# Branch products of a hybrid encoder layer: parts of 768 and 320 tokens, an ungated first state-space half, three PSUM banks beside the scan

## The chip, the cores and the metric

The kernel runs on one core of a Trainium2 chip. The metric is device microseconds for one execution of the whole layer. The kernel before has a median of 2577.64 us over 3 runs (2576.39 to 2583.05); the profiled execution, from which all rows below come, took 2582.58 us with a span of 2580.8 us from its first to its last instruction.

## The reference

One step of a one-layer encoder is computed for 1024 prompt tokens and 64 tokens of a running stream, T = 1088 tokens in all, with a model width of 1024. Cut to what matters here:

```
xn   = rmsnorm(x)
z | xBC | dt | q | k | v | g_ssm | g_att = xn @ w_in
xs, B, C = silu(causal_conv4(xBC))
y_ssm = rmsnorm_by_group( (SSD_scan(xs, dt, B, C) + d * xs) * silu(z) )       # 32 heads in 4 groups, 2048 wide
o     = rmsnorm( softmax(q1 k1) v - lam * softmax(q2 k2) v )                  # 8 heads, 1024 wide
mix   = sigmoid(g_ssm) * (y_ssm @ w_branch_ssm) + sigmoid(g_att) * (o @ w_branch_attn)
x     = x + mix @ w_out
x     = x + ConvFFN(rmsnorm(x))
```

The two branch products and the line `mix` are what the change touches. The kernel keeps tanh(g/2) of each gate, so that sigmoid(g) is (1 + tanh)/2; the factor 1/2 is applied after the output projection.

## The kernel before, in words

Data is kept transposed, with features on the 128 partitions and tokens along the free axis. Every large product is done in three matmuls of a split format: an operand a is rounded to a_hi, a_lo = a - a_hi, and `product` (L140) accumulates hi*hi, hi*lo and lo*hi in one PSUM bank. A weight block (128 x 1024) is loaded by `weights` (L125), cast on ScalarE (L136) and subtracted on VectorE (L137), two blocks deep.

The stages are: input norm, projections of values, queries and keys; attention (L478 on) with the remaining projections as filler; the state-space scan (L640 on) with the rest of the projections and then the branch products as filler; the third branch product; output projection and norm (L789 on); the feed-forward part (L825 on). The emission order gives priorities, and a scheduler decides at compile time in which order each engine's queue holds its instructions. On the chip each queue runs in that order; an instruction that waits holds up all behind it on its engine. All DMAs that matter here go through one queue, SyncE's (SP).

PSUM has eight banks. Two of them (`pm`, tag "mm") serve the large products everywhere; a third group of banks, `more`, is added in the first stage only. The helper `acc` (L112) hands out banks in turn. In the scan the pool `pss` holds six banks of one tile each: `tr` (transposed inputs), `cb` (transposed B, and C times B), `yi` and `ye` (outputs from within the chunk and from the state), `stp` (state update), and `gst` (the sums of squares for the norm by group).

The scan runs over 4 groups and, in each, over three spans of 384, 384 and 320 tokens: 12 spans, numbered 0 to 11. A span has three calls of `step` (L658; 128 tokens each, the last of a group 64) and one of `gated` (L714). A step transposes its inputs into `tr` and `cb`, copies `cb` out on ScalarE (L676), forms the decay matrix on GpSimd and ScalarE (L682, L684), multiplies it on VectorE (L685), and then does `yi`, `ye` and `stp`; VectorE gathers y (L697, L698) and the state (L709). `gated` adds d * xs on VectorE (L718), multiplies by the gate on GpSimd (L719), squares on ScalarE (L720), adds on GpSimd (L721, L722), sums over partitions on TensorE into `gst` (L724), takes the reciprocal root with ScalarE and VectorE (`rstd_of`, L212 to L217; the readers of `gst` are L212 and L214), scales y (L728) and stores it to y_sc. `fill` takes pieces of the filler between steps.

`branch` (L156) does one branch product: the 1088 tokens are cut into halves of 544, each output block m into two slices of 272 columns. It is called three times: for the attention (gated by g, stored to m_sc), for the first half of the state-space input (y_sc rows of groups 0 and 1; gated, m_sc added, stored to n_sc), both as filler in the scan, and for the second half after the scan (gated, n_sc added, split into `mix`). Its gate tiles and the tiles to be added come by DMA into `b_g`; `bring` loads and splits the input of a part. The evacuation of a slice is L196, the addition L198.

## Time and profile before

| | |
|---|---|
| median of 3 runs | 2577.64 us |
| profiled execution | 2582.58 us, span 2580.8 us |
| mean granted TensorE clock | 0.995 |
| VectorE busy | 1399.8 us (54%) |
| ScalarE busy | 1032.2 us (40%) |
| GpSimd busy | 290.0 us (11%) |
| HBM | 263.56 MB read, 100.27 MB written |

A row of the grouped view gives line, engine, operation, output and inputs, shapes and count, then busy time and mean of one in ns, then the engine's idle time just before these instructions and what ended it. A row of the view by windows gives, for a stretch in us from the start of the span, the busy time of each engine with its count of instructions, the granted clock and the share and rate of the DMA engines. Matmuls are pipelined: the duration of one contains the time in which the next is already running, so a rate is read from a count over a stretch. PE is the matrix engine, PEld its weight load, DVE is VectorE, ACT ScalarE, POOL GpSimd.

### The profile page before, as it was taken

The numbers are of one execution on the slowest core, as the hardware profiler recorded it, in microseconds if no ns is written. First come the engines' busy times: TensorE is split into PE (matmuls) and PEld (weight loads), VectorE is DVE, ScalarE is ACT, GpSimd is POOL, SyncE is SP. The second block draws the span as 40 slices with busy tenths as digits, with TensorE's granted clock in tenths as the row PEclk, the third lists the DMA queues.
The fourth block names the chain that finished last, engine by engine and source line by source line (L and its number), as shares of the span: only waits on it lengthen the run. The fifth ranks groups of instructions, "written<-read, shape, count | busy, mean of one in ns | idle before, by whom it ended". The sixth has DMA issues, their size and how long they took to land.

```text
span 2580.8 us, 41810 instructions
## 1 busy us (share of the span) xinstructions
PE 2525.0 (98%) x16484; PEld 2444.8 (95%) x16484; DVE 1399.8 (54%) x2371; ACT 1032.2 (40%) x2113; POOL 290.0 (11%) x387
## 2 busy tenths in 40 slices
PE   8999999999999999999999989999999999999999
PEld 7999999999999999988788879999999999999999
DVE  7326266654447674665679997658333333343333
ACT  5334234544445554565456643335312222131221
POOL 3000001000001110022333430023000000000000
PEclk9999999999999999999999999999999999999999
DMA  5217167545435433176798978555311111111112
GB/s 162 83 54 282 51 257 213 153 142 148 131 126 164 136 112 111 64 232 192 245 332 258 304 246 272 195 187 193 119 42 47 44 42 50 42 50 40 44 43 77
DMA packets 233685, 366.59 MB, mean 142 GB/s; under 512 B 31184, under 2 KB 160464, under 8 KB 233360
## 3 DMA queue, kind: packets, MB, share of 16 engines
q1 hardware_dynamic: 233488, 363.91, 44.2%
q8 instruction: 130, 2.13, 0.3%
q14 instruction: 67, 0.55, 0.1%
HBM read 263.56 MB, written 100.27 MB: 141 GB/s over the span
## 4 chain that ended last, share of the span: by engine, by line
PE 43%; DMA 3%; DVE 3%; ACT 1%; issue 1%; SPq 0%; POOL 0%; DVEq 0%; ACTq 0%; POOLq 0%
PE mm L143 7%; PE mm L145 7%; PE mm L144 7%; PE up L143 7%; PE up L145 7%; PE up L144 7%; DMA in<-x_sc 1%; DMA b_hi<-o_sc 1%; DVE w_lo L137 1%; PE yi L689 1%; PE stp L702 0%; ACT bc L684 0%; DVE y L728 0%; DMA in<-z_sc 0%; DVE b_lo L170 0%
## 5 line engine op out<-in xcount | busy, mean ns | idle before, releaser
L143 PE MATMUL mm<-xn_hi,w_hi 128*128 128x320 f32 (+1 forms) x1496 | 497.9, 333 | 2.3 <-ACT zr L428 1.1
L145 PE MATMUL mm<-xn_hi,w_lo 128*128 128x320 f32 (+1 forms) x1496 | 496.8, 332 | 0.0
L144 PE MATMUL mm<-xn_lo,w_hi 128*128 128x320 f32 (+1 forms) x1496 | 494.6, 331 | 0.0
L136 ACT CAST w_hi<-w_f 128x1024 fp32r<-128x1024 f32 (+2 forms) x220 | 229.3, 1042 | 547.2 <-PE mm L144 369.3
L137 DVE TENSOR_TENSOR w_lo<-w_f,w_hi 128x1024 fp32r<-128x1024 f32 (+2 forms) x220 | 284.9, 1295 | 300.8 <-ACT w_hi L136 298.4
L143 PE MATMUL up<-x_hi,w_hi 128*128 128x384 f32 (+1 forms) x1056 | 345.0, 327 | 2.7 <-ACT x_hi L820 2.7
L144 PE MATMUL up<-x_lo,w_hi 128*128 128x384 f32 (+1 forms) x1056 | 344.8, 327 | 0.0
L145 PE MATMUL up<-x_hi,w_lo 128*128 128x384 f32 (+1 forms) x1056 | 343.3, 327 | 0.0
L143 PEld LDWEIGHTS mm<-xn_hi,w_hi 128*128 128x128 f32 x1496 | 281.9, 188 | 7.9 <-issue 2.8
L145 PEld LDWEIGHTS mm<-xn_hi,w_lo 128*128 128x128 f32 x1496 | 281.6, 188 | 2.9 <-issue 1.9
L144 PEld LDWEIGHTS mm<-xn_lo,w_hi 128*128 128x128 f32 x1496 | 281.8, 188 | 2.6 <-issue 1.3
L143 PE MATMUL mm<-b_hi,w_hi 128*128 128x272 f32 x768 | 228.0, 298 | 19.1 <-DVE b_g L196 15.9
L144 PE MATMUL mm<-b_lo,w_hi 128*128 128x272 f32 x768 | 227.2, 296 | 0.7 <-DMA b_lo<-o_sc 0.7
L145 PE MATMUL mm<-b_hi,w_lo 128*128 128x272 f32 x768 | 227.5, 297 | 0.0
L143 PEld LDWEIGHTS up<-x_hi,w_hi 128*128 128x128 f32 x1056 | 198.7, 188 | 3.1 <-ACT x_hi L820 3.0
L144 PEld LDWEIGHTS up<-x_lo,w_hi 128*128 128x128 f32 x1056 | 198.8, 188 | 0.1
L145 PEld LDWEIGHTS up<-x_hi,w_lo 128*128 128x128 f32 x1056 | 198.5, 188 | 0.0
L880 DVE TENSOR_TENSOR xa<-xa,mm 128x384 f32<-128x384 f32 x144 | 76.5, 531 | 197.3 <-PE mm L145 197.3
L144 PE MATMUL mm<-f_lo,w_hi 128*128 128x384 f32 (+1 forms) x528 | 173.1, 328 | 0.0
L143 PE MATMUL mm<-f_hi,w_hi 128*128 128x384 f32 (+1 forms) x528 | 173.0, 328 | 0.0
L145 PE MATMUL mm<-f_hi,w_lo 128*128 128x384 f32 (+1 forms) x528 | 173.0, 328 | 0.0
L143 PEld LDWEIGHTS mm<-b_hi,w_hi 128*128 128x128 f32 x768 | 147.3, 192 | 25.4 <-DVE b_g L196 15.4
(252 smaller groups left out, 4803.7 us busy)
## 6 DMA issues: line engine op xcount, KB each, us to landing
w_f<-in_win_dram SPq DMA_DIRECT2D x76, 512.0 KB, 4.0
w_f<-in_wup_dram SPq DMA_DIRECT2D x44, 512.0 KB, 3.7
bc<-a_sc SPq DMA_DIRECT2D x32, 512.0 KB, 6.3
w_f<-in_wbs_dram SPq DMA_DIRECT2D x32, 512.0 KB, 4.2
b_g<-g_sc SPq DMA_DIRECT2D x48, 272.0 KB, 4.5
w_f<-in_wout_dram SPq DMA_DIRECT2D x24, 512.0 KB, 3.8
x_sc<-cc SPq DMA_DIRECT2D x48, 192.0 KB, 1.9
kh_t<-k_st SPq DMA_DIRECT2D x32, 272.0 KB, 6.9
```

Of the source, the lines that this page charges most:

```text
L136: S.copy(hi, w)
L137: V.tensor_tensor(out=lo, in0=w, in1=hi, op=ALU.subtract)
L143: PE.matmul(ps, a_hi, b_hi, start=i == 0, stop=False)
L144: PE.matmul(ps, a_hi, b_lo, start=False, stop=False)
L145: PE.matmul(ps, a_lo, b_hi, start=False, stop=i == n - 1)
L689: PE.matmul(yi[u : u + 64, e // 2, :L], xdt[:L, e], bc[:L, e, :L], start=True, stop=True)
L880: V.tensor_tensor(out=xa[:, m, c : c + w], in0=xa[:, m, c : c + w], in1=ps, op=ALU.add)
```

## The change

The branch products are cut into a part of 768 and one of 320 tokens, with slices of 384, 384 and 320 columns. The tiles b_hi and b_lo have one buffer for each part, where two buffers of 544 served both parts in turn. Each tensor that is read beside a product has a tile of its own (768 wide, six buffers, before 1088 wide and four). The second call stores its product without gate and addition, copied out of PSUM by ScalarE. The third call adds n_sc to its product, multiplies by the gate and adds m_sc: three operations on VectorE for each slice. A generator yields after each slice (384 or 320 columns), before after each block (544 columns); still 2.5 pieces are taken per scan step. In the scan `gst` no longer has a bank of its own but takes turns with `cb` in one bank, and the bank set free serves the large products as a third. From the third branch product on, all eight banks serve the large products in turn; before, two served products and five the up-projection.

```diff
+TWO = ((0, 768), (768, 320))
-BG = 4
+BG = 6
-UPB = 5
+BRANCH_STEPS = 2.5
...
-    more, at_bank = None, 0
+    more, at_bank = (None, 0), 0
...
     def acc(w):
         nonlocal at_bank
-        at_bank = (at_bank + 1) % 5
-        pool, tag = (more, "mx") if more is not None and at_bank < 3 else (pm, "mm")
+        pool, n = more
+        at_bank = (at_bank + 1) % (n + 2)
+        pool, tag = (pool, "mx") if at_bank < n else (pm, "mm")
...
+    def branch(stage, side, src, wts, gates, adds, out):
+
+        def octet(x):
+            w = TWO[x][1]
+            return [br.tile([P, 8, w], R32, name=f"{n}{x}", tag=f"{n}{x}") for n in ("b_hi", "b_lo")]
...
+            for a in range(0, w, 384):
+                n = min(384, w - a)
+                t = stage()[:, :n]
+                load(out=t, in_=src[P * k : P * (k + 1), c + a : c + a + n])
+                S.copy(hi[:, k, a : a + n], t)
+                V.tensor_tensor(out=lo[:, k, a : a + n], in0=t, in1=hi[:, k, a : a + n], op=ALU.subtract)
...
-                two = pair()
-                gt, at = two[:, :HALF], two[:, HALF:T]
-                first = load(out=gt, in_=g_sc[g0 + P * m : g0 + P * (m + 1), c : c + HALF])
-                if add is not None:
-                    load(out=at, in_=add[r, c : c + HALF])
+                beside = []
+                for d, r0 in ([(g_sc, gates)] if gates is not None else []) + [(d, 0) for d in adds]:
+                    t = side()[:, :w]
+                    first = load(out=t, in_=d[r0 + P * m : r0 + P * (m + 1), c : c + w])
+                    beside.append(t)
+                to = beside[0] if beside else side()[:, :w]
...
-                for a in (0, HALF // 2):
-                    q = slice(a, a + HALF // 2)
-                    ps = acc(HALF // 2)
+                for a in range(0, w, 384):
+                    q = slice(a, min(a + 384, w))
+                    ps = acc(q.stop - a)
                     product(ps, [(w_hi[:, k], w_lo[:, k], hi[:, k, q], lo[:, k, q]) for k in range(KT)])
                     with tc.high_priority(ahead):
-                        V.scalar_tensor_tensor(gt[:, q], gt[:, q], 1.0, ps, ALU.add, ALU.mult)
-                if add is not None:
-                    V.tensor_tensor(out=gt, in0=gt, in1=at, op=ALU.add)
-                out(m, c, gt)
-                yield
+                        if not beside:
+                            S.copy(to[:, q], ps)
+                        elif not adds:
+                            V.scalar_tensor_tensor(to[:, q], to[:, q], 1.0, ps, ALU.add, ALU.mult)
+                        else:
+                            V.tensor_tensor(out=beside[1][:, q], in0=beside[1][:, q], in1=ps, op=ALU.add)
+                    if adds:
+                        V.scalar_tensor_tensor(to[:, q], to[:, q], 1.0, beside[1][:, q], ALU.add, ALU.mult)
+                        V.tensor_tensor(out=to[:, q], in0=to[:, q], in1=beside[2][:, q], op=ALU.add)
+                    out(m, c + a, to[:, q])
+                    yield
...
     with tc.tile_pool(name="sp", bufs=1) as sp, tc.tile_pool(name="pss", bufs=1, space=PSUM) as pss:
+        more = pss, 1
...
-            ps = pss.tile([P, 512], F32, name="gst", tag="gst")[:, :w]
+            ps = pss.tile([P, 512], F32, name="gst", tag="cb")[:, :w]
...
-            yield from branch(None, pair, o_sc, wba, D, None, store(m_sc))
-            yield from branch(stage, pair, y_sc[:D], wbs[0], 0, m_sc, store(n_sc))
+            yield from branch(None, side, o_sc, wba, D, (), store(m_sc))
+            yield from branch(stage, side, y_sc[:D], wbs[0], None, (), store(n_sc))
...
-            fill(SCAN_STEPS)
+            fill(SCAN_STEPS if late is not None else BRANCH_STEPS)
         load(out=conv, in_=conv_o)
         run(filler)
+    more = None, 0
...
-    run(branch(stage, pair, y_sc[D:], wbs[1], 0, n_sc, mixed))
+    psf = ctx.enter_context(tc.tile_pool(name="psf", bufs=6, space=PSUM))
+    more = psf, 6
+    run(branch(stage, side, y_sc[D:], wbs[1], 0, (n_sc, m_sc), mixed))
...
-            ps = psf.tile([P, 512], F32, name="st2", tag="st2")[:, :w]
+            ps = acc(w)
...
-                ps = psf.tile([P, 512], F32, name="up", tag="up", bufs=UPB)[:, :w]
+                ps = acc(w)
```

More of the change, by code (lines that the diff above doesn't have):

```diff
@@ L154, in project, with bring @@
             yield
-    def branch(stage, pair, src, wts, g0, add, out):
-        def octet():
-            return [br.tile([P, 8, HALF], R32, name=n, tag=n, bufs=2) for n in ("b_hi", "b_lo")]
-        def bring(c, k, hi, lo):
+    def branch(stage, side, src, wts, gates, adds, out):
+        def octet(x):
+            w = TWO[x][1]
+            return [br.tile([P, 8, w], R32, name=f"{n}{x}", tag=f"{n}{x}") for n in ("b_hi", "b_lo")]
+        def bring(x, k, hi, lo):
+            c, w = TWO[x]
             if stage is None:
@@ L162, in bring @@
                 for u, t in enumerate((hi, lo)):
-                    load(out=t[:, k].bitcast(F32), in_=src[D * u + P * k : D * u + P * (k + 1), c : c + HALF])
+                    load(out=t[:, k].bitcast(F32), in_=src[D * u + P * k : D * u + P * (k + 1), c : c + w])
                 return
-            for a in (0, HALF // 2):
-                q = slice(a, a + HALF // 2)
-                t = stage()
-                load(out=t, in_=src[P * k : P * (k + 1), c + a : c + a + HALF // 2])
-                S.copy(hi[:, k, q], t)
-                V.tensor_tensor(out=lo[:, k, q], in0=t, in1=hi[:, k, q], op=ALU.subtract)
@@ L172, in branch @@
-        parts = [octet(), None]
+            for a in range(0, w, 384):
[4 more added lines that the diff above has]
+                V.tensor_tensor(out=lo[:, k, a : a + n], in0=t, in1=hi[:, k, a : a + n], op=ALU.subtract)
+        parts = [octet(0), None]
         for k in range(8):
             bring(0, k, *parts[0])
-        for x, c in enumerate((0, HALF)):
+        for x, (c, w) in enumerate(TWO):
@@ L176, in branch @@
             hi, lo = parts[x]
             if x == 0:
-                parts[1] = octet()
+                parts[1] = octet(1)
             for m in range(KT):
-                r = slice(P * m, P * (m + 1))
-                two = pair()
-                gt, at = two[:, :HALF], two[:, HALF:T]
-                first = load(out=gt, in_=g_sc[g0 + P * m : g0 + P * (m + 1), c : c + HALF])
-                if add is not None:
-                    load(out=at, in_=add[r, c : c + HALF])
+                beside = []
@@ L186, in branch @@
+                for d, r0 in ([(g_sc, gates)] if gates is not None else []) + [(d, 0) for d in adds]:
[3 more added lines that the diff above has]
+                to = beside[0] if beside else side()[:, :w]
                 w_hi, w_lo = weights(wts[m], KT, P)
                 if x == 0 and m >= LAG:
-                    with tc.issue_after(first.ins):
+                    with tc.issue_after(first.ins) if beside else ExitStack():
@@ L189, in branch @@
                         for k in range(8 * (m - LAG) // (8 - LAG), 8 * (m - LAG + 1) // (8 - LAG)):
-                            bring(HALF, k, *parts[1])
-                for a in (0, HALF // 2):
-                    q = slice(a, a + HALF // 2)
-                    ps = acc(HALF // 2)
+                            bring(1, k, *parts[1])
+                for a in range(0, w, 384):
+                    q = slice(a, min(a + 384, w))
+                    ps = acc(q.stop - a)
                     product(ps, [(w_hi[:, k], w_lo[:, k], hi[:, k, q], lo[:, k, q]) for k in range(KT)])
@@ L202, in store @@
+                    if adds:
[3 more added lines that the diff above has]
+                    yield
     def store(dst):
-        return lambda m, c, t: load(out=dst[P * m : P * (m + 1), c : c + HALF], in_=t)
+        return lambda m, c, t: load(out=dst[P * m : P * (m + 1), c : c + t.shape[1]], in_=t)
@@ L225, in hybrid_layer @@
     ps1 = s1.enter_context(tc.tile_pool(name="ps1", bufs=1, space=PSUM))
-    more = s1.enter_context(tc.tile_pool(name="psx", bufs=3, space=PSUM))
+    more = s1.enter_context(tc.tile_pool(name="psx", bufs=3, space=PSUM)), 3
     def stat(w):
@@ L408, in hybrid_layer @@
     s1.close()
-    more = None
+    more = None, 0
     ahead = AHEAD
@@ L750, in stage, with side @@
         def stage():
-            return bs.tile([P, HALF // 2], F32, name="b_f", tag="b_f", bufs=BF)
-        def pair():
-            return bs.tile([P, T], F32, name="b_g", tag="b_g", bufs=BG)
+            return bs.tile([P, 384], F32, name="b_f", tag="b_f", bufs=BF)
+        def side():
+            return bs.tile([P, 768], F32, name="b_g", tag="b_g", bufs=BG)
         def branch_tiles():
@@ L769, in hybrid_layer @@
                 filler, late = late, None
-            fill(SCAN_STEPS)
+            fill(SCAN_STEPS if late is not None else BRANCH_STEPS)
         load(out=conv, in_=conv_o)
         run(filler)
+    more = None, 0
     dq.release()
@@ L779, in mixed @@
     def mixed(m, c, t):
-        q = slice(c, c + HALF)
+        q = slice(c, c + t.shape[1])
         S.copy(mix[0][:, m, q], t)
         V.tensor_tensor(out=mix[1][:, m, q], in0=t, in1=mix[0][:, m, q], op=ALU.subtract)
-    run(branch(stage, pair, y_sc[D:], wbs[1], 0, n_sc, mixed))
+    psf = ctx.enter_context(tc.tile_pool(name="psf", bufs=6, space=PSUM))
+    more = psf, 6
+    run(branch(stage, side, y_sc[D:], wbs[1], 0, (n_sc, m_sc), mixed))
     bs.release()
@@ L791, in hybrid_layer @@
     x2_lo = x2_pool.tile([P, KT, T], R32, name="x2_lo")
-    psf = ctx.enter_context(tc.tile_pool(name="psf", bufs=1, space=PSUM))
     with tc.tile_pool(name="op", bufs=1) as op:
```

## The prediction

> **What bounds the kernel now.** I read the page first, then the view by windows, the waits, and last the rows of the scan one by one.

> ```profile
> span 2580.8 us, 41810 instructions
> PE 2525.0 (98%) x16484; PEld 2444.8 (95%) x16484; DVE 1399.8 (54%) x2371; ACT 1032.2 (40%) x2113; POOL 290.0 (11%) x387
> ```

> TensorE (PE) is busy for 98% of the span, and no other engine comes near. But busy isn't the same as fed at full rate, so the stretches are compared:

> ```profile
> core 0: us, PE busy (x) PEld busy (x) DVE busy (x) ACT busy (x) POOL busy (x), PEclk, DMA share, GB/s
> 1265.00:1420.00 155.00, 145.05 (x1133) 129.45 (x1134) 131.73 (x181) 90.18 (x185) 60.45 (x39) 0.97 0.94 301
> 1420.00:1595.00 175.00, 159.92 (x1246) 144.75 (x1244) 155.72 (x232) 86.86 (x171) 59.44 (x35) 0.98 0.84 274
> 1610.00:1690.00 80.00, 80.00 (x638) 80.00 (x637) 47.95 (x78) 25.40 (x35) 0.00 (x0) 1.00 0.56 184
> 1900.00:2500.00 600.00, 600.00 (x3636) 600.00 (x3635) 216.24 (x327) 138.11 (x213) 21.65 (x64) 1.00 0.15 45
> ```

> The third branch product (1610 to 1690) and the feed-forward part (1900 to 2500) leave PE no gap. The scan with branch products as filler (1265 to 1595) does: PE is busy 305 of 330 us, while VectorE is at 87% and the DMA engines at 0.84 to 0.94. So only the scan and the rate of the matmuls themselves can be improved, and only the scan can easily be made worse. The scan itself runs from its first transposition to its last sum of squares:

> ```profile
> L671 PE MATMUL tr<-con,in x144: 270/273/415, 1116.8 to 1529.4; 128*128 128x128 f32 x128, 128*64 128x128 f32 x16
> L724 PE MATMUL gst<-in,con x24: 430/484/845, 1167.5 to 1566.6; 128*128 128x384 f32 x16, 128*128 128x320 f32 x8
> ```

> From the sum of span 0 (1167.5) to that of span 11 (1566.6) there are 11 spans, so one takes 36.3 us. What PE waits for in it:

> ```profile
> PE mm L143 <- DVE b_g L196: 15.9, 8, 4.6
> PE tr L671 <- ACT in L653: 4.3, 5, 1.6
> PE cb L673 <- ACT b_cb L676: 2.5, 1, 2.5
> PE gst L724 <- POOL in L722: 1.5, 2, 0.9
> ```

> The largest wait is a branch product that finds both banks full because VectorE hasn't emptied one. The scan's own waits are small, since a step of the next span (tr, cb, the decay product) can be done while GpSimd and ScalarE still work on the norm of this one.

> **The change part by part.**

> *Fewer, wider matmuls.* There are 3 x 8 x 8 x 3 = 576 groups of one block, one slice of the contraction and one term. Each had four matmuls of 272 columns and now has 384, 384 and 320, the mix of the feed-forward part. By the windows, 80 us / 638 = 125.4 ns and 600 / 3636 = 165.0 ns. So 4 x 125.4 - 3 x 165.0 = 6.6 ns a group, 576 x 6.6 = 3.8 us saved. [...]

> *A third bank for filler, and ScalarE emptying the second product.* This takes at most the 15.9 us of the wait for L196. Branch 1 is still emptied by VectorE, so I take 14; bounds 0 and 16.

> *Work taken off VectorE.* The second product loses 32 evacuations and 16 additions:

> ```profile
> L196 DVE SCALAR_TENSOR_TENSOR b_g<-b_g,mm 128x272 f32<-128x272 f32 x96 | 41.0, 429 | 46.2 <-PE mm L145 45.5
> L198 DVE TENSOR_TENSOR b_g<-b_g 128x544 f32<-128x544 f32 x32 | 24.5, 764 | 0.7
> PE stp L702 <- DVE xw L681: 0.6, 1, 0.6
> PE yi L689 <- DVE bc L685: 1.6, 1, 1.6
> ```

> That is 32 x 0.429 + 16 x 0.764 = 26 us, and 32 loads of 272 KB fewer in the scan. But beside L196 VectorE ended PE's waits for some 2.5 us only (bc 1.6, xw 0.6, y 0.3), so I take 3 us; bounds 0 and 10. In the third product the additions come back as three operations a slice, 24 x 3 x about 0.55 us = 40 us, where 25 were before; VectorE is at 48 of 80 us there, so they are hidden. Without that cover they would cost the 15 us of difference.

> *The shared bank of `cb` and `gst`.* This is the edit that costs. A bank of one buffer is handed on in emission order, and `gated` of span i is emitted before the steps of span i+1. So the first `cb` of a span now waits until L212 and L214 have read the sum of the span before, and that sum comes only after the whole of `gated`. In the compiled order of the changed kernel every `gst` stands right ahead of the three `cb` of the next span; before, two or three of them stood ahead of it. Each span becomes one chain: cb, three steps, `gated`, gst, next cb. Its length, by the rows of before:

> ```profile
> L685 DVE TENSOR_TENSOR bc<-bc,b_cb 128x1024 f32<-128x1024 f32 x32 | 47.9, 1498 | 7.0 <-ACT b_cb L676 6.4 <-ACT bc L684 0.5
> L681 DVE TENSOR_TENSOR xdt<-tr,dt_tok 128x512 f32<-128x512 f32 x32 | 21.9, 683 | 28.8 <-PE tr L671 28.7
> L709 DVE TENSOR_TENSOR state<-state,stp 128x512 f32<-128x512 f32 x32 | 21.7, 678 | 10.2 <-PE stp L702 5.4 <-POOL state L707 4.9
> L697 DVE TENSOR_TENSOR y<-ye,e 128x512 f32<-128x512 f32 x28 | 19.1, 681 | 6.4 <-PE ye L696 4.9 <-DMA e<-e_sc 1.1 <-PE cb L673 0.4
> L698 DVE TENSOR_TENSOR y<-y,yi 128x512 f32<-128x512 f32 x28 | 19.0, 677 | 4.8 <-PE yi L689 4.8
> L718 DVE SCALAR_TENSOR_TENSOR y<-in,par,y 128x384 f32<-128x384 f32 x32 | 19.0, 653 | 0.1
> L728 DVE SCALAR_TENSOR_TENSOR y<-y,par,grs 128x384 f32<-128x384 f32 x32 | 20.4, 695 | 0.2
> L719 POOL TENSOR_TENSOR y<-y,in 128x1536 f32<-128x1536 f32 x8 | 29.6, 3706 | 11.7 <-DVE y L718 11.7
> L720 ACT ACTIVATE in<-y 128x1536 f32<-128x1536 f32 x8 | 11.9, 1484 | 12.1 <-POOL y L719 12.1
> L721 POOL TENSOR_TENSOR in<-in 128x768 f32<-128x768 f32 x8 | 16.2, 2024 | 1.9 <-ACT in L720 1.9
> L722 POOL TENSOR_TENSOR in<-in 128x384 f32<-128x384 f32 x8 | 10.2, 1270 | 0.5
> L212 ACT ACTIVATE gn<-gst,eps_t x12: 524/574/581, 1171.1 to 1567.3; 128x384 f32<-128x384 f32 x8, 128x320 f32<-128x320 f32 x4
> L214 DVE TENSOR_SCALAR gn<-gst x12: 478/546/558, 1172.3 to 1573.1; 128x384 f32<-128x384 f32 x8, 128x320 f32<-128x320 f32 x4
> ```

> VectorE has in a span three steps of 1.50 + 2 x 0.68 (xdt and xw) + 0.68 x 3 = 4.9 us, then 4 x 0.65 and 4 x 0.70 and four of 0.55 for the root: 14.7 + 2.6 + 2.8 + 2.2 = 22.3 us, nearly all in series, as PE's own parts between them are short. Then come 3.7 + 1.5 + 2.0 + 1.3 = 8.5 us on GpSimd and ScalarE, and the sum with its reader, 0.5 + 0.6. That is 32 us loaded; alone, with less in its way, I estimate 31, and 28 for a span of 320 tokens.

> What this does while there is filler: in the compiled order some 172 wide matmuls stand between two sums, 172 x 165 ns = 28.4 us, and the scan's own work on PE beside them is three steps of

> ```profile
> 1284.58 0.60 PE L671 MATMUL tr<-con,in 128*128 128x128 f32 x4
> 1285.11 1.09 PE L689 MATMUL yi<-bc,xdt 128*64 128x128 f32 x16
> 1288.50 1.05 PE L696 MATMUL ye<-in,state 128*128 128x128 f32 x8
> 1289.64 1.02 PE L702 MATMUL stp<-xw,b_cb 128*128 128x512 f32 x2
> ```

> 3.8 us each, so 40 us in all, against 31 before (150 of 125.4 ns and the same steps). A chain of 32 us fits under 40, but weights, splits and evacuations of the filler stand in the same queues: L214 came 4.8 us after the first sum (1167.5 to 1172.3) and 6.5 after the last (1566.6 to 1573.1). That brings the chain to 37 or 39, plus what the filler's VectorE work adds elsewhere. I take 0.5 us a span over ten spans, 5 us; bounds 0 and 40.

> What it does when the filler is gone: since a span now holds more filler, there is none left after the sum of span 9. The third product can't step in: all but its first slices wait for y_sc of spans 9 and 10, and its six new banks for the last reader of the scan's. So spans 10 and 11 run bare, 31 + 28 = 59 us from the sum of span 9 to that of span 11, with 6 x 3.8 = 23 us of work on PE: 36 us of PE lost. Before, filler covered all of it, and 408 matmuls of the second product were even left after the scan's last step. Bounds 20 (VectorE alone, 2 x 22, less 23) and 45.

> *At no cost.* Eight banks in the feed-forward part: PE is busy 600 of 600 us, nothing to gain, and the operations that empty the banks are the same. Six tiles for neighbours in the place of four: loads run ahead under the products; in the third one some 24 MB in 95 us is 250 GB/s, under the 301 shown above. Parts of one buffer: the next product's part of 768 is loaded under the last 192 matmuls of 320, or under the scan. Up to 8 us if either cover is short; this goes into the range.

> The sum is -4 - 14 - 3 + 36 + 5 = +20 us. On the profiled execution, 2582.6 us, that makes 2602.6; the median of the three runs is 5 lower, so 2598 us.

> **The rivals.**

> *Faster.* The bare span is the point from which it decides. With a bare span of 22 us the tail costs 2 x 22 - 23 = 21 and the sum is -4 - 14 - 3 + 21 + 0 = 0; at 17 us it is -10, and 2568 us. For it: VectorE's means are those of a loaded stretch, and its order may let xdt, xw and the scaling of y slip under GpSimd's part. PE also loses some 25 of 330 us of busy time now, all of which more filler could cover. Against: 8.5 us of GpSimd and ScalarE can't overlap with their own span.

> *No change.* With a bare span of 25 the sum is +6 and the time 2584; that is also what the small terms would give if the spare bank were worth 24.

> *Much slower.* The chain becomes longer than PE's 40 us in every span with filler, as VectorE is at 87% and each of its queued operations delays a link. At 45 us the ten spans add 50 in the place of 5, and the time is 2643 us. For it: the delays of L214 above. Against: VectorE loses 26 us of work, and the next span's steps no longer compete with `gated`.

> *A cold clock.* Between 1304 and 1314 the granted clock is down:

> ```profile
> 1304.00:1314.00 10.00, 9.32 (x58) 0.83 1.05 368
> ```

> PE had just waited 2.5 us for L196. The bare spans will have gaps of 8 us (GpSimd's part), each of which could bring such a drop of some 10 x 0.17 = 1.7 us at full rate, four of them 7 us. [...] The time is then 2605, inside the forecast's own range.

> **How the numbers follow.** The forecast, slower by 8 to 45 us with the cold clock in it, has a chance of 0.46; its own range is 2586 to 2622. Much slower 0.14, no change 0.16, faster 0.24. A measurement of this kernel tells about 0.3%, 8 us, from no change. The range leaves out about a tenth on either side: below 2563 us lies the best part of the faster case, above 2635 us most of the much slower one.

> **What would show it.** Right: PE idle for over 30 us in sum between the sum of span 9 and that of span 11; waits of cb (L673 before) for the readers of `gst`; gaps of GpSimd's length on PE there; the wait for the evacuation in the branch products down to a few us; the third product at 165 ns a matmul without gaps. Wrong: filler left after the last step, sums still 36 us apart or less, or gaps in the third product, which would mean that VectorE, or the neighbours' loads, bound it.

## The result, and the profile after

The changed kernel takes 2641.65 us (median of 4 runs, 2633.9 to 2643.14) against 2578.36 for the kernel before (also 4 runs): a ratio of 1.024, with a 95% interval from 1.0228 to 1.0252. It is 63 us slower. The direction was forecast; the size, 20 us with a range up to 2635, was not.

The page of the changed kernel shows TensorE as the busiest engine still, at 96% of a longer span where it had 98, with 576 matmuls fewer.

```profile
span 2641.3 us, 40581 instructions
PE 2542.7 (96%) x15908; PEld 2448.2 (93%) x15908; DVE 1372.4 (52%) x2331; ACT 1040.6 (39%) x2129; POOL 283.1 (11%) x387
```

The sums of squares of the twelve spans, and their readers, by the view of the tile `gst`:

```profile
L736 PE MATMUL gst<-in,con x24: 430/485/1010, 1171.5 to 1647.8; 128*128 128x384 f32 x16, 128*128 128x320 f32 x8
L223 ACT ACTIVATE gn<-gst,eps_t x12: 522/580/581, 1173.2 to 1648.6; 128x384 f32<-128x384 f32 x8, 128x320 f32<-128x320 f32 x4
L225 DVE TENSOR_SCALAR gn<-gst x12: 483/558/558, 1174.3 to 1649.7; 128x384 f32<-128x384 f32 x8, 128x320 f32<-128x320 f32 x4
```

The last sum comes at 1648, where it came at 1567. Cut at the sum of span 9 (1584), the last sum (1648) and the first matmul of the output projection (1745), the view by windows reads as below; the same cuts in the kernel before follow. Columns are those of the windows in the prediction.

```profile
1119.00:1584.00 465.00, 431.89 (x2784) 391.58 (x2783) 294.83 (x401) 257.02 (x507) 142.99 (x101) 0.96 0.73 232
1584.00:1648.00 64.00, 37.59 (x198) 23.70 (x196) 42.62 (x64) 23.60 (x48) 21.04 (x14) 0.66 0.46 150
1648.00:1745.00 97.00, 94.19 (x553) 92.85 (x552) 67.76 (x121) 30.09 (x47) 0.00 (x0) 0.96 0.64 208
1745.00:1852.00 107.00, 98.96 (x585) 95.83 (x584) 69.70 (x96) 45.25 (x70) 30.77 (x21) 1.00 0.63 203
1950.00:2550.00 600.00, 600.00 (x3637) 600.00 (x3637) 216.47 (x327) 135.74 (x210) 20.83 (x64) 1.00 0.14 45
```

```profile
1117.00:1496.00 379.00, 353.77 (x2599) 316.18 (x2598) 282.74 (x387) 225.68 (x458) 143.26 (x94) 0.98 0.81 258
1496.00:1567.00 71.00, 65.90 (x514) 59.52 (x512) 67.94 (x106) 32.71 (x64) 21.60 (x14) 0.98 0.83 265
1567.00:1691.00 124.00, 121.21 (x960) 120.83 (x960) 74.84 (x124) 38.38 (x57) 0.00 (x0) 1.00 0.65 213
1691.00:1788.00 97.00, 96.47 (x582) 95.40 (x581) 68.39 (x90) 45.67 (x68) 31.67 (x20) 1.00 0.65 215
```

The second row of each is the tail, spans 10 and 11. Before, TensorE did 514 matmuls in 71 us and was busy for 66. Now it does 198 in 64 us, is busy for 38 and idle for 26, and its granted clock has fallen to 0.66. The fourth row is the output projection, which also became 9 us longer, with the same number of matmuls.

TensorE's rows of the tail show the chain of span 10; rows between those shown are left out. Columns are start, duration, engine, line, operation, and in brackets the idle time before it and what ended that.

```profile
1584.25 1.48 PE L736 MATMUL gst<-in,con 128*128 128x384 f32 x2
1587.55 0.47 PE L685 MATMUL cb<-con,in 128*128 128x128 f32 x1 [1.82 <-DVE gn L225]
1591.56 1.98 PE L701 MATMUL yi<-bc,xdt 128*64 128x128 f32 x16
1602.80 1.09 PE L701 MATMUL yi<-bc,xdt 128*64 128x128 f32 x16 [0.48 <-DVE bc L697]
1605.98 0.60 PE L683 MATMUL tr<-con,in 128*64 128x128 f32 x4 [0.82 <-DVE xw L693]
1617.43 1.65 PE L736 MATMUL gst<-in,con 128*128 128x384 f32 x2 [10.85 <-POOL in L734]
1620.89 0.48 PE L685 MATMUL cb<-con,in 128*128 128x128 f32 x1 [1.82 <-DVE gn L225]
```

From sum to sum it is 33.2 us. `cb` waits for the reader of the sum (L225), as the shared bank demands; the three steps follow; then TensorE stands for 10.85 us until GpSimd has added up the squares.

**Where the 60 us of the two profiles lie.** TensorE's own work up to each cut is the filler in the compiled order at 165.0 or 125.4 ns a matmul, plus 3.8 us a step. The rest is called lost: most of it is idle time, and some is work at a halved clock, 0.50 by the view by windows from 1608.0 to 1624.6 (in the tail after, 26 and 12 of the 38 us).

| part | before | after | difference |
|---|---|---|---|
| rate of the branch products | | | -4 |
| lost, first transposition to the sum of span 9 | 379 - 334 = 45 | 466 - 408 = 58 | +13 |
| lost, sum of span 9 to sum of span 11 | 71 - 67 = 4 | 63 - 25 = 38 | +34 |
| lost, last sum to projection | 124 - 120 = 4 | 97 - 91 = 6 | +2 |
| output projection | 97.2 | 106.5 | +9 |
| feed-forward part | 792.4 | 789.6 | -3 |
| start: scan 2 us later, 38 projection matmuls (6 us) after its start that came before it | | | +8 |

The sum is 59 or 60 us. The wait for L196 has gone, as forecast: what L204, VectorE's evacuation in the changed kernel, causes in its place is 3.4 us. But other waits have come up in the spans with filler. These are some of the largest of the changed kernel between 1119 and 1584, and the two of L204:

```profile
PE tr L683 <- DMA in<-x_sc: 6.9, 1, 6.9
PE mx L147 <- DVE w_lo L139: 6.2, 2, 4.1
PE gst L736 <- POOL in L734: 5.2, 2, 3.2
PE stp L714 <- ACT b_cb L688: 5.1, 3, 2.8
PE mx L145 <- ACT w_hi L138: 4.3, 1, 4.3
PE mx L145 <- DVE b_g L204: 1.7, 1, 1.7
PE mm L145 <- DVE b_g L204: 1.7, 1, 1.7
```

### The profile page after: what moved, and what is told of

Its sections match the earlier page's. It is cut to its first block, busy times and chain, and to the rows that moved or that the text cites. A ratio compares the mean times of both kernels' runs of the same rounds, so it can differ in the third digit from the quotient of the medians.

```text
span 2641.3 us, 40581 instructions
## 1 busy us (share of the span) xinstructions
PE 2542.7 (96%) x15908; PEld 2448.2 (93%) x15908; DVE 1372.4 (52%) x2331; ACT 1040.6 (39%) x2129; POOL 283.1 (11%) x387
## 4 chain that ended last, share of the span: by engine, by line
PE 42%; DMA 6%; DVE 4%; ACT 2%; issue 1%; POOL 1%; SPq 0%; DVEq 0%; ACTq 0%; POOLq 0%
PE mx L145 9%; PE mx L147 9%; PE mx L146 9%; PE mm L145 4%; PE mm L147 4%; PE mm L146 4%; DMA in<-x_sc 1%; DMA b_f<-y_sc 1%; PE stp L714 1%; DVE w_lo L139 1%; PE yi L701 1%; PE ye L708 1%; DMA b_g<-n_sc 1%; DMA b_lo<-o_sc 1%; DMA bc<-a_sc 1%
## 5 line engine op out<-in xcount | busy, mean ns | idle before, releaser
L139 DVE TENSOR_TENSOR w_lo<-w_f,w_hi 128x1024 fp32r<-128x1024 f32 (+2 forms) x220 | 280.3, 1274 | 380.9 <-ACT w_hi L138 365.5
L145 PE MATMUL mm<-xn_hi,w_hi 128*128 128x384 f32 (+1 forms) x1416 | 470.1, 332 | 0.0
L147 PE MATMUL mm<-xn_hi,w_lo 128*128 128x384 f32 (+1 forms) x1416 | 467.6, 330 | 0.0
L146 PE MATMUL mm<-xn_lo,w_hi 128*128 128x384 f32 (+1 forms) x1416 | 466.5, 329 | 0.0
L138 ACT CAST w_hi<-w_f 128x1024 fp32r<-128x1024 f32 (+2 forms) x220 | 229.2, 1042 | 496.9 <-PE mx L146 294.2
L145 PEld LDWEIGHTS mm<-xn_hi,w_hi 128*128 128x128 f32 x1416 | 266.6, 188 | 3.6 <-issue 1.8
L145 PE MATMUL mx<-x_hi,w_hi 128*128 128x384 f32 (+1 forms) x784 | 255.1, 326 | 1.7 <-ACT x_hi L834 1.7
L147 PE MATMUL mx<-x_hi,w_lo 128*128 128x384 f32 (+1 forms) x784 | 255.3, 326 | 0.0
L146 PE MATMUL mx<-x_lo,w_hi 128*128 128x384 f32 (+1 forms) x784 | 255.2, 326 | 0.0
L145 PEld LDWEIGHTS mx<-x_hi,w_hi 128*128 128x128 f32 x784 | 147.1, 188 | 2.0 <-ACT x_hi L834 2.0
L146 PEld LDWEIGHTS mx<-x_lo,w_hi 128*128 128x128 f32 x784 | 147.1, 188 | 0.0
L147 PEld LDWEIGHTS mx<-x_hi,w_lo 128*128 128x128 f32 x784 | 147.1, 188 | 0.0
L563 ACT ACTIVATE p_t<-sc,mx 128x1024 f32<-128x1024 f32 (+5 forms) x144 | 106.2, 739 | 93.7 <-DVE mx L554 40.1
L146 PE MATMUL mx<-f_lo,w_hi 128*128 128x384 f32 (+1 forms) x396 | 128.8, 328 | 0.0
L145 PE MATMUL mx<-f_hi,w_hi 128*128 128x384 f32 (+1 forms) x396 | 128.7, 327 | 0.0
L696 ACT ACTIVATE bc<-bc,nacum 128x128 f32<-128x128 f32 (+1 forms) x288 | 86.7, 384 | 70.0 <-POOL bc L694 69.9
L145 PE MATMUL mm<-b_hi,w_hi 128*128 128x384 f32 (+1 forms) x304 | 102.6, 339 | 5.4 <-ACT w_hi L138 2.1
```

The lines of the kernel that those rows point to most:

```text
L138: S.copy(hi, w)
L139: V.tensor_tensor(out=lo, in0=w, in1=hi, op=ALU.subtract)
L145: PE.matmul(ps, a_hi, b_hi, start=i == 0, stop=False)
L146: PE.matmul(ps, a_hi, b_lo, start=False, stop=False)
L147: PE.matmul(ps, a_lo, b_hi, start=False, stop=i == n - 1)
L563: act(p_t[:n, :nk], sc[c][:n, :nk], AF.Exp, bias=mx[:n, c : c + 1], accum_out=dst)
```

## The experiments

Theory A was that the shared bank ties each span to the one before. Its rivals were that the smaller pieces drain the filler whatever the bank (B), and that the third product and its banks lose the time (C). For each run the stages are read from its trace: scan and branch products (first transposition to first matmul of the projection), output projection, feed-forward part. All in us; the ratio is to the kernel before, on the same chip. The medians of the kernel before lay between 2578 and 2584 us beside these runs, so totals of different rows are compared by their ratios. A stage time comes from one execution; executions of the kernel before scatter by 12 us (2572.2 to 2584.6 in the set of e10), so a few us of a stage are not told from noise.

| run | scan and products | projection | feed-forward | median | ratio (95%) |
|---|---|---|---|---|---|
| before | 574.3 | 97.2 | 792.4 | 2578.36 | 1 |
| after | 626.5 | 106.5 | 789.6 | 2641.65 | 1.024 (1.0228 to 1.0252) |
| e1 own bank for gst | 565.1 | 109.1 | 788.5 | 2585.2 | 1.0027 (1.0016 to 1.0039) |
| e2 before, sharing alone | 593.4 | 97.4 | 790.2 | 2603.17 | 1.0095 (1.007 to 1.012) |
| e3 gst shares with ye | 611.2 | 110.4 | 790.1 | 2632.58 | 1.0203 (1.0183 to 1.0222) |
| e4 gst shares with stp | 606.5 | 110.5 | 789.7 | 2629.92 | 1.0196 (1.0171 to 1.0222) |
| e5 sharing, two filler banks | 612.9 | 113.5 | 787.3 | 2630.97 | 1.018 (1.0163 to 1.0197) |
| e6 no sum, three filler banks | 573.9 | 113.8 | 789.6 | 2593.31 | 1.003 (1.0018 to 1.0042) |
| e7 own bank, old banks after the scan | 566.8 | 99.6 | 787.6 | 2574.07 | 0.996 (0.9945 to 0.9974) |
| e8 after, old banks after the scan | 616.6 | 99.9 | 787.5 | 2618.28 | 1.0132 (1.0113 to 1.0151) |
| e9 filler held back | 626.8 | 110.6 | 791.3 | 2643.49 | 1.0242 (1.0224 to 1.0259) |
| e10 e7 with the old gating | 572.1 | 97.4 | 787.6 | 2578.37 | 0.9998 (0.9987 to 1.0009) |
| e11 after, short chain | 629.0 | 108.4 | 789.7 | 2647.64 | 1.0262 (1.0245 to 1.0279) |
| e12 e7, short chain | 574.6 | 99.6 | 787.5 | 2584.35 | 1.0018 (1.0008 to 1.0028) |

### e1: a bank of its own for the sum

```diff
-        more = pss, 1
+        more = None, 0
-            ps = pss.tile([P, 512], F32, name="gst", tag="cb")[:, :w]
+            ps = pss.tile([P, 512], F32, name="gst", tag="gst")[:, :w]
```

> The changed kernel with gst back in a bank of its own, so that the filler has two banks in the scan again; everything else of the change is kept. Theory A (the shared bank of cb and gst ties each span to the one before; its time is 46 us a span with filler, and 63 us for the last two without): spans of 36 us again, filler left after the scan, 2565 to 2590 us. Rival B (the narrower pieces and the ungated second product drain the filler, whatever the bank): over 2615 us. Rival C (the third product with its three VectorE operations a slice and its late banks): what lies after the last sum of squares stays 15 us longer than its matmuls account for, so about 2590 us.

Measured: 2585.2 us. The scan and products take 565.1 us, 61 less than in the changed kernel and 9 less than before. The total is in A's range and the spans take 36 us on average again, so theory A stands for that stage, and B falls: the pieces and the ungated store are those of the changed kernel. The tail is full again, 328 matmuls in 50 us, by the windows of this run:

```profile
1515.00:1565.00 50.00, 48.48 (x328) 43.56 (x327) 39.47 (x55) 25.55 (x48) 22.97 (x12) 1.00 0.56 186
1565.00:1685.00 120.00, 116.42 (x708) 113.86 (x707) 82.19 (x139) 43.51 (x72) 0.00 (x0) 1.00 0.75 246
1685.00:1794.00 109.00, 98.47 (x583) 95.73 (x582) 69.77 (x96) 46.40 (x71) 33.65 (x23) 1.00 0.65 205
```

Rival C had looked for a loss in the third product. There is none from the last sum to the projection (second row: 120 us, before 124), but there is one in the projection itself (third row), which is 12 us longer than before.

### e2: sharing alone, on the kernel before

```diff
-            ps = pss.tile([P, 512], F32, name="gst", tag="gst")[:, :w]
+            ps = pss.tile([P, 512], F32, name="gst", tag="cb")[:, :w]
```

> The kernel before with one edit: gst takes turns with cb in one bank; the bank set free is left empty. Halves of 544, gated second product, two filler banks. Theory A: 40 to 46 us a span, little filler left after the last step, 2610 to 2640 us. Rival B: within 10 us of the kernel before.

Measured: 2603.17 us, 24 us slower (ratio 1.0095), below the figure expected by A and clearly above B's. So the bank alone slows a kernel that has neither the wide pieces nor the third bank. Its scan stage loses 19 us, though, where the same sharing costs 48 between e1 and e5.

### e3 and e4: the sum in another scan bank

```diff
-            ps = pss.tile([P, 512], F32, name="gst", tag="cb")[:, :w]
+            ps = pss.tile([P, 512], F32, name="gst", tag="ye")[:, :w]
```

(in e4 tag="stp")

> The changed kernel with gst in the bank of ye (the output from the state) in the place of cb, three filler banks kept. The first transpositions, C times B and the decay product of the next span no longer wait for the sum. Theory A: between the two, 2600 to 2630 us, with a last span less bare. Rival B: as the changed kernel, 2635 to 2650 us, since the filler has the same three banks and the same pieces.

> The changed kernel with gst in the bank of stp (the state update). The next span can go as far as its first yi before the sum is read. Theory A: 2605 to 2635 us, with filler gone by the sum of span 10 as the compiled order has it. Rival B: as the changed kernel, 2635 to 2650 us.

Measured: 2632.58 and 2629.92 us. e3 falls between the two ranges, 2.6 us above A's; e4 is in A's, near its upper end. The scan stage gains 15 and 20 us on the changed kernel, far from the 61 of e1. Whichever step of the next span is the first to wait for the sum, most of the loss remains.

### e5 and e6: the third bank

e5 keeps the sharing and leaves the bank that it frees empty; e6 has the third bank without sharing. e6 leaves out the sum over partitions, so its output is another one.

```diff
e5
-        more = pss, 1
+        more = None, 0
e6
-            ps = pss.tile([P, 512], F32, name="gst", tag="cb")[:, :w]
-            PE.matmul(ps, ones, zt[:, 0], start=True, stop=True)
+            ps = zt[:, 0]
```

> The changed kernel with gst and cb still sharing a bank, but with the third bank for the filler left empty in the scan. Theory A (sharing is the cause, the third bank neither helps nor hurts): the scan and the three products take 620 to 630 us as in the changed kernel, 2630 to 2645 us in all. Theory A2 (the third bank adds to the loss, since the run with sharing alone on the kernel before lost only 24): 2605 to 2615 us.

> The changed kernel with the third filler bank, but without the sum over partitions of the group norm: the root is taken of each partition's own sum, so no bank and no 12 matmul pairs of gst are needed and cb shares with nothing (the output is then another one). Theory A: spans of 36 us or less, 2570 to 2590 us; a third bank without sharing is then worth what lies below the 2585 of gst in its own bank, less some 8 us for the sums left out. Theory A2 (the third bank itself drains the filler early): 2600 us or more.

Measured: e5 2630.97 us, at the lower edge of A's range, with a stage below A's 620 to 630; A2's 2605 to 2615 is far off. e6 2593.31 us lies between its two ranges. In the scan stage, sharing without the third bank costs 612.9 - 565.1 = 48 us, and the third bank another 626.5 - 612.9 = 14; the ratios, 1.018 and 1.024, are clear of each other. In e6 the stage is 9 us longer than in e1, though 12 sums were left out, but the ratios of the two, 1.003 and 1.0027, don't tell them apart. So the third bank gains nothing in either setting; that it costs something is shown for the shared form only. The wait that it was to remove had gone without it: in e1, with two banks, evacuations cost TensorE 3.7 us.

```profile
PE mm L145 <- ACT b_g L202: 1.9, 1, 1.9
PE mm L145 <- DVE b_g L204: 1.8, 2, 1.4
```

In e6 the largest wait of TensorE is another: transpositions that wait for the activated input of the next span, whose loads are late (ScalarE waits 40.5 us for them in e6, 26.9 in e1).

```profile
PE tr L683 <- ACT in L665: 18.4, 5, 6.8
PE stp L714 <- ACT b_cb L688: 9.6, 3, 4.2
```

### e7 and e8: the banks after the scan

Both give the third product and the projection two banks, the sum of the second norm one of its own, and five more to the feed-forward part alone. e7 starts from e1, e8 from the changed kernel.

```diff
-    psf = ctx.enter_context(tc.tile_pool(name="psf", bufs=6, space=PSUM))
-    more = psf, 6
     run(branch(stage, side, y_sc[D:], wbs[1], 0, (n_sc, m_sc), mixed))
...
+    psf = ctx.enter_context(tc.tile_pool(name="psf", bufs=5, space=PSUM))
...
-            ps = acc(w)
+            ps = psf.tile([P, 512], F32, name="st2", tag="st2", bufs=1)[:, :w]
             PE.matmul(ps, ones, s1_t, start=True, stop=True)
...
     mix_pool.release()
+    more = psf, 5
```

> The kernel with gst in its own bank, and the stage after the products with banks as before: two for the third product and the output projection, one for the sum of the norm, and five more for the feed-forward part alone, seven in all there. If the 12 us that the output projection lost (109 us in the place of 97) come from the sum of the norm taking its turn among the eight banks, it is back at 97 to 99 us and the whole at 2570 to 2576 us, below both kernels. If they come from the third product's operations on VectorE, it stays at 107 to 110 and 2583 to 2587 us.

> The changed kernel with cb and gst sharing and three filler banks, but the stage after the scan with banks as before (two for the third product and the output projection, one for the sum, seven in the feed-forward part). If the banks cost 9 us in the output projection: 2630 to 2635 us. If the handover of the scan's banks to the third product matters as well, since it can now start earlier on the two it has: 2622 to 2630 us. If neither: 2640 us.

Measured: e7 2574.07 us, ratio 0.996 (0.9945 to 0.9974), 0.4% faster than the kernel before; e8 2618.28 us, ratio 1.0132 against the changed kernel's 1.024. The projection is back at 99.6 and 99.9 us. What TensorE waits for in the projection of e1 (first fence) and in that of e7 (second):

```profile
PE mx L828 <- POOL s L826: 9.2, 3, 3.1
PE mx L147 <- DVE w_lo L139: 0.7, 2, 0.4
PE mm L147 <- DVE w_lo L139: 0.6, 1, 0.6
```

```profile
PE mm L145 <- DVE x L818: 1.2, 1, 1.2
PE mm L147 <- DVE w_lo L139: 1.2, 2, 0.7
```

In e1 the sum of the norm stands in TensorE's queue before GpSimd has added up its squares, three times for about 3 us. In the changed kernel this happens once (3.1 us); 5.0 us more of its 9 are waits for the split weights (L138 and L139). e8 gains 10 us more in the scan and products (616.6 against 626.5): there the third product starts on the two banks that it has, and needn't wait for the scan's. 72 of its matmuls come before the last sum, 24 in the changed kernel.

### e9: filler held back for the tail

```diff
+                late_part = hold if x == 1 and m in (0, 4) and not beside else []
+                with tc.issue_after(late_part[m // 4].ins) if late_part else ExitStack():
+                    w_hi, w_lo = weights(wts[m], KT, P)
...
+                last = V.scalar_tensor_tensor(y[:, j], y[:, j], col(O_SN + 4 * g + j), rs, ALU.mult, ALU.mult)
+            if g == 3 and c < 768:
+                hold.append(last)
```

> The changed kernel; the part of 320 of the second product is held back: its weight blocks 0 to 3 are loaded only after the last scaling of span 9, blocks 4 to 7 after that of span 10. The compiled order then has span 9 bare and 14 and 18 us of filler in spans 10 and 11, which were bare; the work is the same. Theory P (a span with filler takes TensorE's own work, 40 us, and some 6 us of waits; a bare one takes its chain, about 32 us): span 9 goes from 52 to about 33 us, spans 10 and 11 stay at 30 to 35, the whole at 2620 to 2628 us. Theory Q (a span with any filler takes a chain of 45 us, since the filler's operations delay its links): spans 10 and 11 go from 33 and 30 to 40 or more, the whole at 2640 us or above.

Measured: 2643.49 us, as the changed kernel. Span 9 fell from 52.2 to 37.4 us, but spans 10 and 11 rose from 33.2 and 29.9 to 40.1 and 40.0: 117 us for the three in the place of 115. Their windows (span 9, 10, 11 of e9):

```profile
1530.00:1567.00 37.00, 17.92 (x106) 12.18 (x104) 22.79 (x36) 22.23 (x46) 13.12 (x9) 0.73 0.55 170
1567.00:1607.00 40.00, 29.64 (x197) 24.04 (x197) 24.13 (x35) 21.90 (x43) 13.79 (x9) 0.84 0.59 184
1607.00:1647.00 40.00, 33.54 (x198) 27.67 (x199) 27.25 (x38) 12.59 (x21) 9.68 (x5) 0.81 0.65 223
```

Theory Q said so, and theory P's 2620 to 2628 us is missed. The bare tail isn't the fault of where the filler ran out: a span of about 32 us takes 40 once it gets 14 or 18 us of filler, so a good half of the filler lengthens it.

### e10: what the ungated store is worth

e10 is e7 with the old order of gate and addition; the second product is gated and gets m_sc, the third n_sc.

```diff
-            yield from branch(stage, side, y_sc[:D], wbs[0], None, (), store(n_sc))
+            yield from branch(stage, side, y_sc[:D], wbs[0], 0, (m_sc,), store(n_sc))
...
-    run(branch(stage, side, y_sc[D:], wbs[1], 0, (n_sc, m_sc), mixed))
+    run(branch(stage, side, y_sc[D:], wbs[1], 0, (n_sc,), mixed))
...
+                        V.scalar_tensor_tensor(to[:, q], to[:, q], 1.0, ps, ALU.add, ALU.mult)
+                    if adds:
+                        V.tensor_tensor(out=to[:, q], in0=to[:, q], in1=beside[1][:, q], op=ALU.add)
```

> The kernel with gst in its own bank and the old banks after the scan (2574 us, 0.996 of before), with the old gating: the second product is multiplied by its gate and gets m_sc added, the third gets n_sc alone. If the ungated store is worth the 3 us of VectorE's waits and more: 2576 to 2580 us, the scan and products 3 to 6 us longer. If the gain of that kernel is due to the parts of 768 and 320 alone: within 2 us of 2574.

Measured: 2578.37 us, ratio 0.9998. The scan and products are 5.3 us longer than in e7, as expected, the projection 2.2 shorter. The total is in the range given for a store worth more than VectorE's 3 us. So the ungated store is worth some 5 us in the stage, and the wider parts at most a few. TensorE's wait for evacuations is 6.2 us here and 2.8 in e7, against 15.9 in the kernel before: the wide parts and their tiles took the larger share of it away.

### e11 and e12: a shorter chain

TensorE sums the four squared tiles itself, in the shared form (e11) and in e7 (e12).

```diff
-            G.tensor_tensor(out=zt[:, 0:2], in0=zt[:, 0:2], in1=zt[:, 2:4], op=ALU.add)
-            G.tensor_tensor(out=zt[:, 0], in0=zt[:, 0], in1=zt[:, 1], op=ALU.add)
...
-            PE.matmul(ps, ones, zt[:, 0], start=True, stop=True)
+            for j in range(4):
+                PE.matmul(ps, ones, zt[:, j], start=j == 0, stop=j == 3)
```

> The changed kernel, with the two additions of GpSimd ahead of gst taken out: TensorE sums the four squared tiles itself, in four accumulating matmuls in the place of one. That takes 3.3 us (2.0 and 1.3) out of the chain of a span and adds about 1 us of TensorE work to it. Theory Q (each span is one chain from cb to gst): 2 to 3 us a span shorter, 24 to 36 us over twelve, 2605 to 2618 us. Theory P (a span with filler is bound by TensorE's work): the two bare spans alone gain, the ten others lose 1 us each, 2640 to 2648 us.

> The same edit in the kernel with gst in its own bank and the old banks after the scan (2574 us). There gst is on no chain between spans. Theory Q: no gain, 2570 to 2582 us, with the 12 us of added matmuls either in idle time or paid for.

Measured: e11 2647.64 us, no faster than the changed kernel (ratios 1.0262 and 1.024, whose intervals overlap), and e12 2584.35, 2 us above its range and 0.6% slower than e7 by the ratios. e12's stage is 8 us longer than e7's, so most of the 12 us of added matmuls is paid for, as where TensorE is the bound. e11 misses theory Q's range and lies in P's, but not by P's mechanism: its two tail spans did not gain, they took 71 us where the changed kernel takes 63. Averaged over the spans, the link from the last yi to the sum did shrink, from 17.9 to 14.4 us, but the one from the sum to the next first yi grew from 12.7 to 15.9. TensorE's rows show what came into it. The sum has six matmuls more, 1 us. The compiled order also moved filler there: between the sum and the next first yi stand 68 filler matmuls on average over spans 0 to 8, where the changed kernel has 61, and 53 behind span 9, where it has none. So the run changed more than the chain, and doesn't test theory Q cleanly.

## Why the prediction was wrong in size

**Right: the bound, the serial spans, the tail.** The chain of a bare span was put at 31 and 28 us; it took 33.2 and 29.9. The tail was put at 36 us of TensorE lost; it lost 34 more than before. That is close in part by luck: some 12 us of it are work that took longer under the halved clock, which the forecast's sum left out, and TensorE was idle for 26 us there, not for the "over 30" that was named as a sign. Of the other signs, waits of `cb` for the readers of `gst` (3.6 us), the gap of GpSimd's length and the short wait for evacuations came. The 408 matmuls that the prediction found left after the scan's last step are those behind its last transposition; 335 of the second product stand behind the step's last matmul. That the sum and `cb` follow each other strictly is in the rows, and e1, which undoes it together with the third bank, takes 61 us out of the stage.

**Wrong: the spans with filler.** The sum had -14 for the third bank, -3 for VectorE and +5 for the chain under filler, so 45 us of lost time would have become 33. It became 58. The step that failed is "A chain of 32 us fits under 40": filler was taken to lie beside the chain, but TensorE's queue holds both in one order. On average over the spans the first yi of the next span came 5 us before the sum in the kernel before and 12.7 us after it in the changed one, and a span took 45.9 us where TensorE's work is 40. The rows show where the filler stands. Between the sum and the next first yi, spans 0 to 8 have 54 to 75 filler matmuls, 61 on average or 10 us; this link takes 13.9 us there, and 7.3 and 7.4 us behind spans 9 and 10, where no filler stands in it. For the sum of span 4 the view by windows, from the sum's end to the next first `cb` and on to the first yi, has TensorE busy all the time (31 and 33 of the matmuls are filler). So less is left to cover the norm: from the end of the last yi to the sum there are 84 filler matmuls on average in spans 0 to 9, 14 us of work for a link of 17.8.

```profile
1351.50:1356.80 5.30, 5.30 (x33) 1.00 0.82 246
1356.80:1364.10 7.30, 7.30 (x42) 1.00 1.05 384
```

e9 shows it by experiment: filler put into a bare span lengthens it by a good half of its own length. The -14 failed too. The wait for an evacuation went, but the third bank gains nothing: e5, without it, is 0.6% faster than the changed kernel.

**Wrong: eight banks "at no cost".** Only the feed-forward part was looked at. It gained 3 us, but with the old banks it takes no longer (787.6 and 787.5 us in e7 and e8). The projection between was passed over; it lost 9 us there and 12 to 17 in e1 and e3 to e6. e7 and e8 put that down to the banks after the scan. The handover of banks to the third product was seen, but only in the tail's account; e8 puts it at 10 us.

**The rivals.** "Much slower" gave 2643 us and a span of 45, both close to what was measured. Its price of 50 us for these spans was too high, though: with its -14 and -3 it comes to 33 us, and the lost time there rose by 13. It left out the projection and the later start, so its time was hit by errors that cancel. The cold clock was sized at 7 us. In the changed kernel the clock was halved for 90 us between the first transposition and the projection, 17 before. TensorE was busy for 60 us of that, 16 before. At a clock of 0.50 the 272-column matmuls of the branch products start 0.227 us apart in the kernel before, at 1.00 0.126 us, so at most half of this busy time is loss: 30 us against 8, and up to 22 of the 52 lost in that stage are its part. That is an estimate, a bound from the two traces.

The prediction counted the four gaps of the tail alone. In the trace nine halvings begin in the stage, and they last 3.41, 6.83, 13.65, 17.07 or 23.89 us each. None of the nine follows 3.41 us, the length of the shortest, without a matmul: TensorE was busy for 18 to 49% of the 3.41 us before each. At 1304, in the kernel before, it had waited for 2.5 us, and around the gap of 10.85 us the halving began 1.0 us into the gap, after a stretch (first row) in which TensorE was busy for 1.58 of 3.41 us:

```profile
1604.18:1607.59 3.41, 1.58 (x12) 1.15 (x12) 3.41 (x7) 2.85 (x9) 1.42 (x2) 1.00 0.56 142
1607.00:1625.00 18.00, 5.29 (x14) 2.58 (x16) 6.63 (x12) 5.54 (x15) 6.98 (x4) 0.53 0.07 15
1631.00:1655.00 24.00, 16.23 (x55) 11.84 (x56) 15.90 (x27) 5.79 (x10) 6.54 (x4) 0.51 0.24 80
```

Seven of the nine halvings begin in spans with filler, for which the prediction counted none.

**What stays open.** Sharing costs 48 us on the structure of the changed kernel and 19 on that of the kernel before. The halved clock (85 us in e5, 51 in e2) and the third product, which in e5 waits for the scan's banks (none of its matmuls comes before the last sum, 72 in e2), both point that way, but neither was tried alone. Nor was the chain shortened with the filler left where it stood: in e11 both changed. And what the halved clock costs is bounded by the traces only, as no run took it away.

## What to carry to other kernels

A buffer of one that two stages share is a dependence between iterations, here at 48 us (e5 against e1): find out how far the next iteration had been ahead at that place, and price the whole chain that can no longer overlap, not the wait alone. Filler on an in-order queue doesn't lie beside such a chain; look in the compiled order at how much of it stands between two links. In e9 a good half of it was added to the chain: 14 and 18 us of filler took spans of 33.2 and 29.9 us to 40.1 and 40.0. A bank, or a buffer, is worth only what the wait for it costs once the other edits are in: the wait of 15.9 us was 6.2 with the wide parts alone (e10) and 2.8 with the ungated store beside them (e7), and e7, which keeps both and gives back the banks, is 0.4% faster than the kernel before.
